# The low part behind the sums, and another order of pairs, in the output product of a short-convolution layer

## The chip, the cores and the metric

The kernel runs on one core of one Trainium2 chip. The metric is device time in microseconds (us), the median of several executions of the whole program. A second figure, the span, comes from one profiled execution: the time from the first to the last recorded instruction. The engines that matter are TensorE (PE in the profile, with its weight loads as PEld), VectorE (DVE), ScalarE (ACT) and SyncE (SP), whose queue issues the transfers from device memory. Each engine works off its own queue of instructions in the order of the built program, and semaphores tell it when what another engine or a transfer must have finished is done.

## What is computed

The reference, cut to one layer as it is run here (256 tokens, model width D = 2048, inner width E = 4096):

```python
h = rmsnorm(x, norm_g)
shift, scale, gate = split(silu(c) @ ada_w + ada_b, 3)
h = h * (1 + scale) + shift
b_gate, c_gate, v, g = split(h @ w_in, 4)              # w_in: D x 4E
y = b_gate * causal_conv3(c_gate * v) * silu(g)        # 256 tokens x E
out = rmsnorm(x + gate * (y @ w_out), final_g)         # w_out: E x D
```

The two big products are `h @ w_in` and `y @ w_out`. Everything is float32 and the products must keep more than one reduced-precision pass gives.

## The kernel before

**Three products for one.** TensorE multiplies operands of the type `float32r`. So each float32 operand is split into a high part (a cast to `float32r`, on ScalarE) and a low part (the operand less its high part, on VectorE), and a product is the sum of three: high by high, high by low, low by high. For the weights this split is the work of `split`: `split_hi` (L341) casts a loaded tile of 128 x 2048 on ScalarE, `split_lo` (L346) subtracts on VectorE. `triple` (L695) issues the three matmuls, each 128 x 128 by 128 x 512.

**Stages.** First come the norms, the modulation and the product with `w_in` (lines up to L657), whose results `y` are kept split in 16 tiles, `ys[0]` to `ys[15]`; one tile holds a pair of 128-row blocks of E. Then comes `y @ w_out`. Its first half, output columns 0 to 1023, is the loop over `order` at the end of which the change sits; it takes the 16 pairs one by one. Its second half, columns 1024 to 2047, is the loop `for dc in range(2, 4)` behind it, with the accumulator tile `mm_o`.

**Plain pairs.** For a plain pair `j` (0 to 9) the loop loads a tile `raw_o` with the two blocks of `w_out` (`load_o`, L684, 1 MB), splits it, and issues 24 matmuls, 8 triples, into the accumulators `wide[0]` and `wide[1]` (`mm_w` in the profile).

**Seven-product pairs.** Pairs 10 to 15 (`SEVEN`) go through `seven`, which needs 7 triples, 21 matmuls, in place of 8, in the manner of Strassen: it multiplies sums of blocks by sums of tokens. The token sums (`form`) were made earlier in `token_forms`. The weight sums are made here. The tile `raw_o` is seen as four blocks of 128 x 512. VectorE makes four sums `s` of them (`sums_o`) in three instructions: one for two sums at once (L720, 128 x 1024), then L722 and L723 (128 x 512 each, each reading what the one before wrote). ScalarE casts blocks 1 to 3 as loaded (L721, 128 x 1536), VectorE takes their low part `bl` (L724), and then the four sums are split like any tile: a cast on ScalarE (L341, 128 x 2048) and a low part on VectorE (L346, 128 x 2048). Three of the seven triples use the blocks as loaded, four use the sums; they accumulate into `wide`, `p75` (`mm`), `p1` and `p6` (`mm` as well in the profile, since buffer numbers are left out).

**Gather.** When the last seven-product pair has been issued, `gather` (L738 to L746) adds the accumulators `p1`, `p6` and `p75` up: one copy on ScalarE (L742) and four additions of 128 x 512 on VectorE (L741). The last three additions read `p75`. The accumulator `mm_o` of the next stage takes the place in PSUM that `p75` had, so its first matmul must wait for the last of them.

**Buffers.** The working tiles lie in nine buffers of 128 x 2048, three each of the kinds `raw`, `hi` and `lo`, handed out in turn. In this loop `raw_o` and `sums_o` take `lo` buffers, high parts take `hi` buffers, low parts take `raw` buffers. A plain pair so uses one buffer of each kind, a seven-product pair two of each. A load waits until the last reader of the third tile before it in its kind is done; a cast waits until TensorE has done with the third high part before.

**Order of the work.** A scheduler in the build orders the instructions of each engine from the order in which they are traced, their priorities and its own idea of their durations; what it has put down is then fixed. `tc.add_manual_dep(a, b, ...)` with the class `NoSync` only says that `a` is to stand behind `b` on their engine, and adds no semaphore. The order of the pairs is written out by hand in `order`.

Of the kernel before, what the change touches and what calls it, by code (L numbers as in the profile page):

```python
# [8 lines left out]
F32 = mybir.dt.float32  # L9
F32R = mybir.dt.float32r  # L10
AF = mybir.ActivationFunctionType
ALU = mybir.AluOpType
# [105 lines left out]
def short_conv_layer(ctx: ExitStack, tc: tile.TileContext, x, c, norm_g, ada_w, ada_b, w_in, conv_w, w_out, final_g, out):  # L118
    nc = tc.nc
# [25 lines left out]
    def w_tile(kind, name, dtype=F32, i=None):  # L145

        if i is None:
            i = nth[kind] % 3
            nth[kind] += 1
        return wpool.tile([P, SLOT], dtype, tag=f"{kind}{i}", name=name, bufs=1)  # L150
# [12 lines left out]
    after = mybir.DependencyInfo(mybir.DependencyClass.NoSync, mybir.DependencyReason.DATA)  # L163
# [111 lines left out]
    for t in range(TT):  # L275
        for dh in range(2):
# [3 lines left out]
            else:  # L280
                nc.vector.scalar_tensor_tensor(
                    out=junk[:, t], in0=xt[t][dh], scalar=1.0, in1=xt[t][dh], op0=ALU.mult, op1=ALU.mult,
# [50 lines left out]
    def hi_tile():  # L333
        return w_tile("hi", "hi", F32R)

    def lo_tile(lo_tag="lo"):
        return w_tile(lo_tag, "lo", F32R)
# [23 lines left out]
    def split(raw, n, lo_tag="lo"):  # L361

        return split_lo(raw, n, split_hi(raw, n), lo_tag)
# [64 lines left out]
    sums = {}  # L428
# [139 lines left out]
    def gate(dc):  # L568
        return gates[dc // 2][:, dc % 2, :]
# [119 lines left out]
    def y_parts(ct, t):  # L689
        return [ys[ct // 2][:, ct % 2, h, t * P : (t + 1) * P] for h in range(2)]  # L690

    def triple(dst, y, hi, lo, opens=False, ends=False):

        for i, (a, b) in enumerate(((0, hi), (0, lo), (1, hi))):
            nc.tensor.matmul(dst, y[a], b, start=opens and i == 0, stop=ends and i == 2, skip_group_check=True)  # L695
# [17 lines left out]
    def seven(j, raw):  # L713


        opens, last = j == SEVEN[0], j == SEVEN[-1]
        sums = w_tile("lo", "sums_o")
        hi, lo = hi_tile(), lo_tile("raw")
        b, s, bh, bl = (v.rearrange("p (b f) -> p b f", f=W) for v in (raw, sums, hi, lo))
        nc.vector.tensor_tensor(out=s[:, 0:2], in0=b[:, 1:3], in1=b[:, 0:1].to_broadcast([P, 2, W]), op=ALU.subtract)  # L720
        nc.scalar.copy(bh[:, 1:4], b[:, 1:4])  # L721
        nc.vector.tensor_tensor(out=s[:, 2], in0=b[:, 2], in1=s[:, 0], op=ALU.add)  # L722
        nc.vector.tensor_tensor(out=s[:, 3], in0=b[:, 3], in1=s[:, 2], op=ALU.subtract)  # L723
        nc.vector.tensor_tensor(out=bl[:, 1:4], in0=b[:, 1:4], in1=bh[:, 1:4].bitcast(F32), op=ALU.subtract)  # L724
        sh, sl = (v.rearrange("p (b f) -> p b f", f=W) for v in split(sums, SLOT, "raw"))

        def f(i):
            return [forms[j][h][:, i] for h in range(2)]

        triple(p1, y_parts(2 * j, 0), bh[:, 1], bl[:, 1], opens, last)  # L730
        triple(wide[0][:, 1], y_parts(2 * j + 1, 0), bh[:, 3], bl[:, 3])
        triple(wide[0][:, 0], f(3), bh[:, 2], bl[:, 2])
        triple(p75[:, 0], f(2), sh[:, 1], sl[:, 1], opens, last)
        triple(p75[:, 1], f(0), sh[:, 0], sl[:, 0], opens, last)
        triple(p6, f(1), sh[:, 2], sl[:, 2], opens, last)
        triple(wide[1][:, 1], y_parts(2 * j + 1, 1), sh[:, 3], sl[:, 3])
# [8 lines left out]
        add(ends[0][:, 0], p75[:, 1], u2)  # L745
        add(ends[1][:, 0], p75[:, 1], ends[1][:, 1])  # L746

    order = (0, 1, 10, 2, 11, 3, 12, 4, 13, 5, 14, 6, 15, 7, 8, 9)
    for n, j in enumerate(order):
        raw = w_tile("lo" if n else "raw", "raw_o")  # L750
        load_o(raw, 2 * j, 2, 0, 2 * W)
        load_ends(n - 4)
        if j in SEVEN:
            seven(j, raw)
            if j == SEVEN[-1]:
                gather()
            continue
        hi, lo = split(raw, SLOT, "raw")
        for t in range(TT):
            for k in range(2):  # L760
                for d in range(2):
                    o = slice((k * 2 + d) * W, (k * 2 + d + 1) * W)
                    triple(
                        wide[t][:, d], y_parts(2 * j + k, t), hi[:, o], lo[:, o],
                        n == 0 and k == 0, j == order[-1] and k == 1,
                    )
# [24 lines left out]
    for dc in range(2, 4):  # L791
# [16 lines left out]
        for ep in range(n_ep):  # L808
# [3 lines left out]
            if dc == 3:  # L812
# [3 lines left out]
                    out=raw3, in0=raw3, in1=gate(dc).unsqueeze(1).to_broadcast([P, EP, W]), op=ALU.mult  # L816
# [45 lines left out]
```

## Time and profile before

| what | us |
|---|---|
| median of three executions (911.7 to 912.86) | 911.83 |
| the profiled execution, its own time | 911.95 |
| span of that execution | 910.2 |
| TensorE busy in the span | 894.2 |
| VectorE busy | 653.5 |
| ScalarE busy | 476.1 |

How to read the views: a timeline row gives the start of an instruction in us from the start of the span, its duration, engine, line of the kernel, operation, what it writes and reads without buffer numbers, and in square brackets how long its engine had been idle before it and what ended that. "x2" merges two neighbours of a kind. A windows row gives the busy time and number of instructions of each engine in a stretch, then the clock granted to TensorE and the share of the transfer engines. Matmuls overlap: the distance from start to start, and not the duration, is what one costs.

### The profile page before, as it was taken

The page shows a single profiled execution, that of the slowest core. Times are in us where ns is not written, and L with a number is a line of the kernel's source. Part 1 is how long each engine was busy: PE and PEld are TensorE (multiplying, and loading weights), DVE is VectorE, ACT ScalarE, POOL GpSimd, SP SyncE. Part 2 cuts the span into 40 slices and gives each one's busy share as a digit, 9 for nine tenths or more (in the row PEclk, how much of TensorE's full clock was granted, in tenths as well). Part 3 has the DMA queues.
Part 4 walks back from the last instruction along what each step waited for, and adds up shares of the span by engine and source line. Part 5 has one row for each costly group of instructions (what it writes and reads, how often), then busy time and mean ns, then how long its engine had stood idle before and what let it go on. Part 6 is the DMA issues. An engine that isn't in the chain of part 4 may idle for free.

```text
span 910.2 us, 16272 instructions
## 1 busy us (share of the span) xinstructions
PE 894.2 (98%) x7029; PEld 854.7 (94%) x7029; DVE 653.5 (72%) x647; ACT 476.1 (52%) x422; POOL 0.7 (0%) x6
## 2 busy tenths in 40 slices
PE   6999999999999999999999999999999999999996
PEld 4999999999999999999999999999999987788885
DVE  4889899889888886665555686555555577887882
ACT  6768866665558765643333434343444335544343
POOL 0000000000000000000000000000000000000000
PEclk9999999999999999999999999999999999999998
DMA  9999999999998686676666887656666486685542
GB/s 313 367 371 349 364 309 365 346 370 359 345 327 282 184 301 189 189 241 202 202 186 186 259 273 231 201 185 194 185 193 197 137 307 191 209 293 185 185 138 93
DMA packets 159656, 227.65 MB, mean 250 GB/s; under 512 B 5680, under 2 KB 104160, under 8 KB 159200
## 3 DMA queue, kind: packets, MB, share of 16 engines
q1 hardware_dynamic: 159456, 226.56, 75.7%
q8 instruction: 55, 0.90, 0.4%
q14 instruction: 17, 0.14, 0.0%
q10 hardware_dynamic: 128, 0.04, 0.0%
HBM read 224.49 MB, written 2.10 MB: 249 GB/s over the span
## 4 chain that ended last, share of the span: by engine, by line
PE 98%; ACT 1%; DMA 1%; ACTq 0%; issue 0%; DVE 0%
PE mm_b L471 38%; PE mm_s L471 38%; PE mm_o L695 10%; PE mm_w L695 7%; PE mm L695 2%; PE tp_idle L258 1%; DMA rows<-in_ada_b_dram 1%; PE sum L380 1%; PE ps_gate L596 0%; PE tp_g L461 0%; PE tp_x L310 0%; ACT hi L341 0%; ACT acc L492 0%; ACT hT L327 0%; ACT mm_s L504 0%; ACT big L787 0%
## 5 line engine op out<-in xcount | busy, mean ns | idle before, releaser
L471 PE MATMUL mm_s<-hT,hi 128*128 128x256 f32 x2048 | 350.4, 277 | 0.1
L471 PE MATMUL mm_b<-hT,hi 128*128 128x256 f32 x2048 | 349.4, 276 | 0.0
L471 PEld LDWEIGHTS mm_s<-hT,hi 128*128 128x128 f32 x2048 | 308.5, 188 | 1.0 <-ACT hT L327 0.3
L471 PEld LDWEIGHTS mm_b<-hT,hi 128*128 128x128 f32 x2048 | 308.2, 188 | 0.5 <-issue 0.5
L471 PE MATMUL mm_b<-hT,lo 128*128 128x256 f32 x1024 | 282.6, 276 | 0.0
L471 PE MATMUL mm_s<-hT,lo 128*128 128x256 f32 x1024 | 282.2, 277 | 0.0
L346 DVE TENSOR_TENSOR lo<-raw,hi 128x2048 fp32r<-128x2048 f32 (+1 forms) x66 | 148.0, 2243 | 113.6 <-ACT hi L341 113.2
L341 ACT CAST hi<-raw 128x2048 fp32r<-128x2048 f32 (+1 forms) x66 | 123.7, 1874 | 193.9 <-PE mm_b L471 152.6
L471 PEld LDWEIGHTS mm_b<-hT,lo 128*128 128x128 f32 x1024 | 192.2, 188 | 0.5 <-issue 0.5
L471 PEld LDWEIGHTS mm_s<-hT,lo 128*128 128x128 f32 x1024 | 191.7, 188 | 0.3 <-DVE lo L346 0.2
L346 DVE TENSOR_TENSOR lo<-raw_s,hi 128x2048 fp32r<-128x2048 f32 (+1 forms) x80 | 147.6, 1850 | 32.8 <-ACT hi L341 32.0
L341 ACT CAST hi<-raw_s 128x2048 fp32r<-128x2048 f32 (+1 forms) x80 | 124.0, 1559 | 72.9 <-PE mm_s L471 59.6
L454 DVE SCALAR_TENSOR_TENSOR gv<-at,silu_c,gv 128x512 f32<-128x512 f32 x105 | 78.6, 749 | 6.3 <-DMA at<-in_ada_w_dram 4.5
L341 ACT CAST hi<-raw_o 128x2048 fp32r<-128x2048 f32 x26 | 49.6, 1906 | 60.6 <-PE mm_o L695 36.6
L695 PE MATMUL mm_o<-hi,y 128*128 128x512 f32 x256 | 78.7, 389 | 0.0
L346 DVE TENSOR_TENSOR lo<-raw_o,hi 128x2048 fp32r<-128x2048 f32 x26 | 59.5, 2290 | 24.2 <-ACT hi L341 24.1
L492 ACT COPY acc<-mm_s 128x1024 f32<-128x1024 f32 x54 | 54.6, 1012 | 34.7 <-PE mm_s L471 34.7
L695 PE MATMUL mm_w<-hi,y 128*128 128x512 f32 x184 | 58.2, 390 | 0.0
L695 PEld LDWEIGHTS mm_o<-hi,y 128*128 128x128 f32 x256 | 48.0, 188 | 9.9
L695 PE MATMUL mm_o<-lo,y 128*128 128x512 f32 x128 | 49.5, 389 | 0.0
L593 DVE SCALAR_TENSOR_TENSOR gacc<-at_g,silu_c,gacc 128x512 f32<-128x512 f32 x60 | 45.0, 749 | 5.6 <-DMA at_g<-in_ada_w_dram 4.6
L695 PEld LDWEIGHTS mm_w<-hi,y 128*128 128x128 f32 x184 | 34.5, 188 | 7.7 <-ACT hi L341 0.2
(142 smaller groups left out, 512.6 us busy)
## 6 DMA issues: line engine op xcount, KB each, us to landing
raw<-in_sc_w_in_dram SPq DMA_DIRECT2D x64, 1024.0 KB, 5.6
raw_s<-in_sc_w_in_dram SPq DMA_DIRECT2D x47, 1024.0 KB, 8.5
raw_o<-in_sc_w_out_dram SPq DMA_DIRECT2D x32, 1024.0 KB, 5.1
at<-in_ada_w_dram SPq DMA_DIRECT2D x114, 256.0 KB, 8.4
raw_s<-in_sc_w_in_dram SPq DMA_DIRECT2D x33, 512.0 KB, 6.9
at_g<-in_ada_w_dram SPq DMA_DIRECT2D x32, 512.0 KB, 7.6
at<-in_ada_w_dram SPq DMA_DIRECT2D x6, 512.0 KB, 9.4
x<-in_x_dram SPq DMA_DIRECT2D x4, 512.0 KB, 6.1
```

What stands on the lines that cost most here:

```text
L258: nc.tensor.matmul(tp_idle, ident, ones[:, 0:1].to_broadcast([P, 512]), start=True, stop=True)
L341: nc.scalar.copy(hi[:, :n], raw[:, :n])
L346: nc.vector.tensor_tensor(out=lo[:, :n], in0=raw[:, :n], in1=hi[:, :n].bitcast(F32), op=ALU.subtract)
L380: nc.tensor.matmul(sums0[:, o * P : (o + 1) * P], rows[:, o // NK0, (o % NK0) * P : (o % NK0 + 1) * P], col.to_broadcast([P, P]), start=k ...
L454: nc.vector.scalar_tensor_tensor(out=gv, in0=at4[:, i], scalar=c_k, in1=gv, op0=ALU.mult, op1=ALU.add)
L471: mm = last_mm[0] = nc.tensor.matmul(dst, w, h[k], start=begins and left, stop=ends, skip_group_check=True)
L492: nc.scalar.copy(acc[ch, q], bank)
L593: nc.vector.scalar_tensor_tensor(out=ga, in0=at3[:, i, :], scalar=s, in1=ga, op0=ALU.mult, op1=ALU.add)
L695: nc.tensor.matmul(dst, y[a], b, start=opens and i == 0, stop=ends and i == 2, skip_group_check=True)
```

## The change

Two things, both in the first half of `y @ w_out`.

In `seven`, a dependency of the class `NoSync` puts the low part `bl` of the blocks as loaded (L724) behind the last of the three instructions that make the sums (L723). Before, the scheduler was free to set L724 between them.

In `order`, the six seven-product pairs and the ten plain ones follow each other otherwise. Before, from the third place on, they alternate strictly and three plain pairs stand at the end (7, 8, 9). After, two plain pairs stand together at 2, 3 and at 5, 6, the others alternate, and one plain pair (9) stands behind the last seven-product pair (15).

```diff
-        nc.vector.tensor_tensor(out=s[:, 3], in0=b[:, 3], in1=s[:, 2], op=ALU.subtract)
-        nc.vector.tensor_tensor(out=bl[:, 1:4], in0=b[:, 1:4], in1=bh[:, 1:4].bitcast(F32), op=ALU.subtract)
+        all_sums = nc.vector.tensor_tensor(out=s[:, 3], in0=b[:, 3], in1=s[:, 2], op=ALU.subtract)
+        low = nc.vector.tensor_tensor(out=bl[:, 1:4], in0=b[:, 1:4], in1=bh[:, 1:4].bitcast(F32), op=ALU.subtract)
+        tc.add_manual_dep(low.ins, all_sums.ins.name, after, reason="the sums' cast runs beside the low part")
...
-    order = (0, 1, 10, 2, 11, 3, 12, 4, 13, 5, 14, 6, 15, 7, 8, 9)
+    order = (0, 1, 10, 2, 3, 11, 4, 12, 5, 6, 13, 7, 14, 8, 15, 9)
```

The number of loads, casts, additions and matmuls is the same in both. In the built program of after, the VectorE queue reads so from pair 13 on (the pair in brackets):

```
L724 low part as loaded (13), L346 low part of sums (13),
L720 first sums (14), L346 low part (7), L722 (14), L723 (14), L724 (14), L346 low part of sums (14),
L720 first sums (15), L346 low part (8), L722 (15), L723 (15), L724 (15), L346 low part of sums (15),
L346 low part (9), first addition of gather, L346 low part (first tile of mm_o),
second and third addition of gather, L346 low part (second tile of mm_o), last addition of gather
```

For the earlier pairs L720 stands behind the low part of the plain pair before it, as it does throughout in before. In before, all four additions of `gather` stand together, behind the low parts of pairs 7 and 8 and ahead of that of pair 9.

## Prediction

> **What bounds the kernel now.** I read the page first, then the busy time by windows, then the timelines of TensorE, VectorE and ScalarE through the stage that the change touches, and last the transfers.
>
> ```profile
> span 910.2 us, 16272 instructions
> ...
> PE 894.2 (98%) x7029; PEld 854.7 (94%) x7029; DVE 653.5 (72%) x647; ACT 476.1 (52%) x422; POOL 0.7 (0%) x6
> ...
> PEclk9999999999999999999999999999999999999998
> ...
> PE 98%; ACT 1%; DMA 1%; ACTq 0%; issue 0%; DVE 0%
> ```
>
> TensorE is the bound, nearly without a gap and at full clock, and the chain that ended last lies on it. So the edit is worth what it adds to or takes from TensorE's waits. The windows show where there are any:
>
> ```profile
> 760.00:770.00 10.00, 9.97 (x43) 7.72 (x42) 7.92 (x6) 5.19 (x3) 0.00 (x0) 1.00 0.58 186
> 780.00:790.00 10.00, 10.00 (x43) 7.75 (x43) 7.92 (x7) 5.19 (x3) 0.00 (x0) 1.00 0.62 204
> 800.00:810.00 10.00, 10.00 (x46) 8.26 (x45) 9.13 (x7) 3.95 (x3) 0.00 (x0) 1.00 0.89 319
> 900.00:910.00 10.00, 2.74 (x13) 1.93 (x11) 2.62 (x6) 3.74 (x8) 0.00 (x0) 0.75 0.59 211
> ```
>
> Where pairs alternate, TensorE issues 43 matmuls in 10 us, later 46: small stalls that "busy" hides, since matmuls overlap. The timeline sizes them:
>
> ```profile
> 730.63 0.39 PE L695 MATMUL mm_w<-hi,y 128*128 128x512 f32 x1
> ...
> 754.68 0.40 PE L695 MATMUL mm<-lo,form 128*128 128x512 f32 x1
> ...
> 786.55 0.50 PE L695 MATMUL mm<-lo,form_g 128*128 128x512 f32 x1
> ...
> 797.23 0.50 PE L695 MATMUL mm<-lo,form_h 128*128 128x512 f32 x1
> ...
> 810.55 0.39 PE L695 MATMUL mm_o<-hi,y 128*128 128x512 f32 x1
> ...
> 815.54 0.39 PE L695 MATMUL mm_w<-hi,y 128*128 128x512 f32 x1
> 815.77 0.39 PE L695 MATMUL mm_o<-lo,y 128*128 128x512 f32 x1
> ...
> 820.53 0.39 PE L695 MATMUL mm_o<-lo,y 128*128 128x512 f32 x1
> ```
>
> From 815.77 to 820.53 stand 21 matmuls without a wait: 0.2267 each. A plain pair is 24 of them, 5.44 us; a seven-product pair 21, 4.76. The stage, from 730.63 to 815.77, holds 10 x 24 + 6 x 21 = 366 and the one `mm_o` issued early, at 810.55: 367 x 0.2267 = 83.2 us, and takes 85.14. So its stalls come to **1.95 us**, and that is all there is to gain. They come with a period: from 786.55 to 797.23 a plain and a seven-product pair take 10.68 against 10.20.
>
> What sets 10.68 is a loop through VectorE and ScalarE:
>
> ```profile
> 745.91 1.22 DVE L720 TENSOR_TENSOR sums_o<-raw_o 128x1024 f32<-128x1024 f32 x1
> 747.17 0.69 DVE L722 TENSOR_TENSOR sums_o<-raw_o,sums_o 128x512 f32<-128x512 f32 x1
> ...
> 773.52 2.29 DVE L346 TENSOR_TENSOR lo<-sums_o,hi 128x2048 fp32r<-128x2048 f32 x1 [2.05 <-ACT hi L341]
> 775.73 2.28 DVE L346 TENSOR_TENSOR lo<-raw_o,hi 128x2048 fp32r<-128x2048 f32 x1
> 777.94 1.22 DVE L720 TENSOR_TENSOR sums_o<-raw_o 128x1024 f32<-128x1024 f32 x1
> 779.07 1.75 DVE L724 TENSOR_TENSOR lo<-raw_o,hi 128x1536 fp32r<-128x1536 f32 x1
> 780.74 0.69 DVE L722 TENSOR_TENSOR sums_o<-raw_o,sums_o 128x512 f32<-128x512 f32 x1
> 781.47 0.69 DVE L723 TENSOR_TENSOR sums_o<-raw_o,sums_o 128x512 f32<-128x512 f32 x1
> 784.20 2.29 DVE L346 TENSOR_TENSOR lo<-sums_o,hi 128x2048 fp32r<-128x2048 f32 x1 [2.05 <-ACT hi L341]
> ```
>
> ```profile
> 782.27 1.91 ACT L341 CAST hi<-sums_o 128x2048 fp32r<-128x2048 f32 x1 [3.98 <-DVE sums_o L723]
> ...
> 787.44 1.48 ACT L721 CAST hi<-raw_o 128x1536 fp32r<-128x1536 f32 x1 [1.47 <-DMA raw_o<-in_sc_w_out_dram]
> ...
> 815.97 1.91 ACT L341 CAST hi<-raw_o 128x2048 fp32r<-128x2048 f32 x1 [3.76 <-PE mm_w L695]
> ```
>
> VectorE works 8.63 us of a period and stands idle 2.05, while ScalarE casts the sums (1.91). From 773.52 to 784.20 is the same 10.68 as TensorE's.
>
> **The low part behind the sums.** Nothing is added or removed: L724 (1.75) now runs beside the cast. The sums go 1.26 (745.91 to 747.17), 0.73, then L724 starts 0.60 after L723; the cast starts 0.11 after L723's end and ends 0.69 + 0.11 + 1.91 = 2.71 after its start, L724 at 2.35. VectorE's idle time falls from 2.05 to 0.4, its period to about 9.1, below the 10.20 that TensorE needs. That takes the 1.95 away. Nothing waits longer for L724 itself: TensorE reads it first among the pair's low parts, but the sums were what came late. What is late next is a transfer, below.
>
> **The order of the pairs.** Matmuls, casts and loads are as many as before and the 16 loads keep their places on SP's queue. Plain pairs put earlier give VectorE room (2.2 us for 5.44 of TensorE). Two new things come in at the end, both out of the order in which the VectorE queue is built.
>
> *First wait: the low part of pair 8.* In the queue of after, L720 of pairs 14 and 15 stands ahead of the low part of plain pairs 7 and 8. L720 waits for its load, and that load has the buffer which L724 of the pair before gives free. So a loop closes: L724 (14) ends, load (15), L720 (15), low part (8). The load:
>
> ```profile
> L684 SPq DMA_DIRECT2D raw_o<-in_sc_w_out_dram x32: 367/368/379, 707.8 to 875.2; - x32
> ...
> DMA to landing us min/median/max: 5.0/5.1/7.6
> ```
>
> L723 ended at 781.47 + 0.69 = 782.16 and released a load whose cast began at 787.44: 5.28 for ScalarE. For VectorE I take 5.2. From L720 (14) to L720 (15): 1.13 + 2.21 + 0.73 + 0.60 + 1.75 + 5.2 = 11.6 us, where TensorE needs 10.2. VectorE's own sum of 9.1 no longer decides; it now idles for a transfer.
>
> Whether that shows depends on the lead before it, so I follow the chain from where it hangs on TensorE. Without stalls pair 3 ends after 117 matmuls, at 730.63 + 26.52 = 757.15, and frees the buffer for the cast of pair 4; a waiter starts 0.43 after the last matmul's start (815.54 to 815.97), so at 757.35. Then: low part (4) 1.95 later, 759.30; L720 (12) 761.51; L722 762.77; L723 763.50; L724 764.10, done 765.85; load of 6 and its cast 5.28 later, 771.13; low part (6) 773.06; L720 (13) 775.27; L724 (13) 777.86, done 779.61; load of 14; L720 (14) 784.81; low part (7) 785.94 to 788.23. TensorE wants it after another 135 matmuls from 757.15 and the three of pairs 7 and 14 that need no low part, at 788.43: just in time. A round later the low part (8) ends at 788.23 + 11.6 = 799.83 and is wanted at 788.43 + 10.20 = 798.63. **Wait: 1.2 to 1.3 us.**
>
> *Second wait: the accumulator of the next stage.* `mm_o` needs the place of `p75`, which `gather` reads. In before it was read long ahead:
>
> ```profile
> 804.30 0.68 DVE L741 TENSOR_TENSOR z<-mm,z 128x512 f32<-128x512 f32 x1
> 804.90 2.28 DVE L346 TENSOR_TENSOR lo<-raw_o,hi 128x2048 fp32r<-128x2048 f32 x1
> ```
>
> The last addition ended at 804.98, 5.6 before the first `mm_o` at 810.55. In after only pair 9 stands behind pair 15, and the last addition is queued behind the low parts of two tiles of the next stage. TensorE goes on at about 799.9, has 22 matmuls of pair 8 left (to 804.9), 20 of 15 and 24 of 9: ready for `mm_o` at 814.9. VectorE: cast of pair 9 when pair 8 ends, 805.1; low part (9) 807.0; first addition 809.2; low part 809.8 (or 0.2 later, for its own load); two additions at 812.2; low part 813.4; last addition 815.6, done 816.3. **Wait: 1.4 to 1.6 us.** Both waits start a matmul stream anew, which before costs 0.11 each time (matmuls of 0.50 at 786.55 and 797.23 against 0.39).
>
> **The sum.** 1.3 + 1.5 + 0.2 - 1.95 = +1.05. On the profiled execution, 911.95, that is 913.0; on the median, which is 0.12 lower, **912.9 us** (+0.12%). Behind `mm_o`'s first matmul VectorE and ScalarE have slack, so it is all there is.
>
> The load's time carries both signs. With 5.0, the least that the trace has, both rounds shorten by 0.1 or 0.2: first wait 1.0, sum +0.7. The Trainium skill ("DMA: Bandwidth & Descriptors", Anatomy of one DMA) fits a transfer as about 2.0 us and its bytes at 436 GB/s, measured for transfers that GpSimd issues; an estimate from it for 1 MB is 4.4 us, by which the first wait would vanish and the sum be -0.35, so 911.5. This case's loads take 5.0 to 5.2 where they stand alone, so the trace decides. The other end is crowded loads:
>
> ```profile
> L684 SPq DMA_DIRECT2D raw_o<-in_sc_w_out_dram x1: 367/367/367, 802.5 to 802.5; - x1
> ...
> DMA to landing us min/median/max: 6.5/6.5/6.5
> ```
>
> **The rivals.**
>
> *Crowded loads, slower.* The load of 15 is issued about 3 us behind that of 8, and the first of the next stage 3 us behind that of 9. If the distance is too short, each is up to 6.5 - 5.1 = 1.4 late, and adds that to its wait: +1.05 + 2.8 = up to 915.7, and 914.2 if it is half. It decides from 0.4 us each on, where the sum passes 0.2%. For it: the row above, behind another load. Against: loads 4 us apart took 5.1. Chance 0.25.
>
> *One wait only.* If the load is 0.6 quicker than I take it, or the lead at pair 7 is a microsecond more, the first wait goes: -1.95 + 1.5 + 0.1, 911.5. It is where the fit of the Trainium skill leads. Against: the chain hangs on TensorE and on rows that repeat. Chance 0.10.
>
> *Neither wait, faster.* The dependency does what it is for and TensorE catches up with nothing: 911.83 - 1.95 = 909.9. It needs the last addition of `gather` 1.5 earlier, against its place in the queue. Chance 0.05.
>
> *The clock falls after a wait.* The window from 900 shows 0.75 where TensorE stands idle most of the time; 2.5 us in 10. After each of two waits that would be +5: 918. Against: stalls in before leave 1.00. Chance 0.02. The Trainium skill ("TensorE: Matmul & The Clock Gate", HAM oscillation) speaks of idle gaps over about 3.4 us, which these are not.
>
> That the dependency does nothing is excluded: in the built queue L724 stands behind L723 in all six pairs.
>
> **How the numbers follow.** 0.2% of 911.83 is 1.8 us, about what a measurement of this kernel tells from no change. My forecast has 0.58, with its own range 912.3 to 913.6. Within 0.2% lie it, less a little at its upper end, and the one-wait case: 0.65. Slower are the crowded loads, the clock and that upper end: 0.30. Faster: 0.05. The range runs from the one-wait case, 911.3, to the crowded loads at somewhat over half, 914.5, and leaves out the faster case, the clock and the worst of the loads.
>
> **What would show it.** VectorE's wait before the low part of the sums near 0.4 in place of 2.05; no stalls of TensorE through pair 13; one of 1.2 to 1.3 at the first low part of pair 8, VectorE having waited over 2 us for a load before L720 of 14 and 15; one of 1.4 to 1.6 before the first `mm_o`. I am wrong if the load of 15 takes over 5.5, if pair 7 already waits, or if a wait of TensorE stands in a place not named here.

## The result and the profile after

The changed kernel takes 914.18 us in the median, against 911.83 before: a ratio of 1.0025, with a 95% interval from 1.0017 to 1.0034. So it is slower by 2.35 us, a quarter of a per cent. (One execution of 2351.95 us is left out.) The profiled execution took 914.21 us with a span of 912.4.

First the page of after, the chain that ended last, by engine:

```profile
PE 88%; DMA 5%; DVE 3%; ACT 2%; issue 1%; SPq 1%; ACTq 0%; DVEq 0%
```

Before, 98% of it lay on TensorE; now it leaves TensorE and runs through transfers, VectorE and ScalarE. These shares say what the chain runs through, not how long TensorE waits, which is far less. They say that TensorE waits somewhere, and that what it waits for hangs on a load. The windows of after say where (columns as before: busy time and count for TensorE, its weight loads, VectorE, ScalarE and GpSimd, then clock and transfers):

```profile
760.00:770.00 10.00, 10.00 (x46) 8.29 (x45) 8.35 (x7) 4.12 (x3) 0.00 (x0) 1.00 0.67 213
...
810.00:820.00 10.00, 8.16 (x35) 6.15 (x34) 10.00 (x10) 5.67 (x5) 0.00 (x0) 1.00 0.83 278
```

From 760 to 770 TensorE issues 46 matmuls where it issued 43: the small stalls are gone. Later there are real gaps, and from 810 to 820 VectorE is busy all the time while TensorE issues 35. The timeline of TensorE in after sizes them (in after the lines of `gather` stand one lower, so L742 is the addition that was L741):

```profile
730.05 0.39 PE L695 MATMUL mm_w<-hi,y 128*128 128x512 f32 x1
...
787.64 0.39 PE L695 MATMUL mm<-hi,y 128*128 128x512 f32 x1
788.25 0.50 PE L695 MATMUL mm_w<-lo,y 128*128 128x512 f32 x1 [0.23 <-DVE lo L346]
...
798.36 0.39 PE L695 MATMUL mm<-hi,y 128*128 128x512 f32 x1
800.04 0.50 PE L695 MATMUL mm_w<-lo,y 128*128 128x512 f32 x1 [1.30 <-DVE lo L346]
...
809.51 0.86 PE L695 MATMUL mm_w<-hi,y 128*128 128x512 f32 x3
810.61 0.50 PE L695 MATMUL mm_w<-lo,y 128*128 128x512 f32 x1 [0.24 <-DVE lo L346]
...
815.50 0.39 PE L695 MATMUL mm_w<-hi,y 128*128 128x512 f32 x1
817.50 0.47 PE L695 MATMUL mm_o<-hi,y 128*128 128x512 f32 x1 [1.60 <-DVE z L742]
```

From 730.05 to 787.64 lie 254 steps of 0.2267 us, 57.58 in 57.59: no stall up to pair 13 and into pair 7. Then four waits. Each is the distance from the start before, less 0.2267: 0.38 at pair 7, 1.45 at pair 8, 0.42 at pair 9 (the last of the three at 809.51 starts at 809.96) and 1.77 at the first `mm_o`: 4.02. With the restarts and some hundredths, the stage's 366 matmuls (82.97) take 87.45 from 730.05 to 817.50, so 4.48 stand beside them where 1.95 stood. That is 2.53 more. TensorE reached the stage 0.58 earlier (730.05 against 730.63; a second trace of after, below, has 730.46, so this varies from one execution to the next) and what is behind it took 0.24 longer; together 2.2, as the spans say.

The timeline of VectorE in after, with L724 of pair 12 and then the end of the stage:

```profile
763.56 1.75 DVE L724 TENSOR_TENSOR lo<-raw_o,hi 128x1536 fp32r<-128x1536 f32 x1
...
784.77 1.22 DVE L720 TENSOR_TENSOR sums_o<-raw_o 128x1024 f32<-128x1024 f32 x1 [2.66 <-DMA raw_o<-in_sc_w_out_dram]
785.91 2.28 DVE L346 TENSOR_TENSOR lo<-raw_o,hi 128x2048 fp32r<-128x2048 f32 x1
...
789.44 1.75 DVE L724 TENSOR_TENSOR lo<-raw_o,hi 128x1536 fp32r<-128x1536 f32 x1
791.58 2.29 DVE L346 TENSOR_TENSOR lo<-sums_o,hi 128x2048 fp32r<-128x2048 f32 x1 [0.38 <-ACT hi L341]
796.56 1.23 DVE L720 TENSOR_TENSOR sums_o<-raw_o 128x1024 f32<-128x1024 f32 x1 [2.70 <-DMA raw_o<-in_sc_w_out_dram]
797.71 2.28 DVE L346 TENSOR_TENSOR lo<-raw_o,hi 128x2048 fp32r<-128x2048 f32 x1
```

The dependency does its work: 0.38 idle before the low part of the sums at 791.58, where 2.05 stood. But VectorE now stands 2.66 and 2.70 before L720 of pairs 14 and 15, for their loads, and the low parts of pairs 7 and 8 are queued behind it. What ScalarE did at that time shows what this costs (the timeline of ScalarE in after):

```profile
770.94 1.91 ACT L341 CAST hi<-raw_o 128x2048 fp32r<-128x2048 f32 x1 [1.78 <-DMA raw_o<-in_sc_w_out_dram]
...
793.61 1.91 ACT L341 CAST hi<-raw_o 128x2048 fp32r<-128x2048 f32 x1 [2.07 <-PE mm_w L695]
...
806.32 1.91 ACT L341 CAST hi<-raw_o 128x2048 fp32r<-128x2048 f32 x1 [2.98 <-DMA raw_o<-in_sc_w_out_dram]
```

The high part of pair 8 was ready at 793.61 + 1.91 = 795.52, and its low part started at 797.71, though VectorE had nothing to do until 796.56. The Trainium skill ("TensorE: Matmul & The Clock Gate", Architectural detail: the array is 16x 32x32, not 1x 128x128) calls the queues of ScalarE and VectorE strictly first in, first out; this trace agrees, with an idle engine for 1.04 us ahead of work that was ready.

The fourth wait is at `gather`. VectorE in after, from the low part of pair 9 to the last addition:

```profile
808.26 2.29 DVE L346 TENSOR_TENSOR lo<-raw_o,hi 128x2048 fp32r<-128x2048 f32 x1 [2.59 <-ACT hi L341]
...
811.07 2.28 DVE L346 TENSOR_TENSOR lo<-raw_o,hi 128x2048 fp32r<-128x2048 f32 x1
813.27 1.28 DVE L742 TENSOR_TENSOR z<-mm,big 128x512 f32<-128x512 f32 x2
814.47 2.28 DVE L346 TENSOR_TENSOR lo<-raw_o,hi 128x2048 fp32r<-128x2048 f32 x1
816.66 0.68 DVE L742 TENSOR_TENSOR z<-mm,z 128x512 f32<-128x512 f32 x1
```

VectorE has no idle time from 808.26 on. Its last addition ends at 816.66 + 0.68 = 817.34, behind the low parts of two tiles of the next stage, and the first `mm_o` starts at 817.50.

### The profile page after: what moved, and what is told of

Its sections match the earlier page's. It is cut to its first block, busy times and chain, and to the rows that moved or that the text cites. A ratio compares the mean times of both kernels' runs of the same rounds, so it can differ in the third digit from the quotient of the medians.

```text
span 912.4 us, 16272 instructions
## 1 busy us (share of the span) xinstructions
PE 892.8 (98%) x7029; PEld 854.9 (94%) x7029; DVE 653.6 (72%) x647; ACT 476.9 (52%) x422; POOL 0.7 (0%) x6
## 4 chain that ended last, share of the span: by engine, by line
PE 88%; DMA 5%; DVE 3%; ACT 2%; issue 1%; SPq 1%; ACTq 0%; DVEq 0%
PE mm_b L471 38%; PE mm_s L471 36%; PE mm_o L695 10%; PE mm_w L695 3%; DMA raw_o<-in_sc_w_out_dram 2%; DMA raw_s<-in_sc_w_in_dram 2%; DVE lo L346 1%; ACT hi L341 1%; DMA at<-in_ada_w_dram 1%; SPq L231 1%; DMA x<-in_x_dram 1%; DVE lo L724 1%; PE ps_gate L596 0%; PE tp_g L461 0%; PE mm L695 0%
```

## The experiments

Theory A, from the prediction: two places in VectorE's built queue cost the time, L720 ahead of the low part of pairs 7 and 8 (first wait), and the last addition of `gather` behind two low parts (second wait). The dependency by itself is a gain. The rivals blame the order of pairs itself, through loads that come closer together, or the dependency. Where a kernel's timeline is shown, the first `mm_w` and the first `mm_o` bound the stage; 82.97 of what lies between is matmuls.

### Each half alone

The dependency with the old order:

```diff
-    order = (0, 1, 10, 2, 3, 11, 4, 12, 5, 6, 13, 7, 14, 8, 15, 9)
+    order = (0, 1, 10, 2, 11, 3, 12, 4, 13, 5, 14, 6, 15, 7, 8, 9)
```

> The dependency alone, with the order of pairs of before. Theory A (the dependency takes the stalls away, the order of the pairs puts new ones in): no stall of TensorE in the stage, since VectorE's period falls to about 9.1 us against TensorE's 10.2, L720 stands behind the low part of the plain pair throughout, and three plain pairs stand behind the gather; 911.83 - 1.95 = 909.9, between 909.4 and 910.4. Theory B (the late low part of the blocks as loaded is itself what costs, because TensorE reads it first in a pair): the small stalls only move to the first low part of each seven-product pair, 911.8 or above.

Measured: 910.21 us, ratio to before 0.9981 (0.9972 to 0.9990). TensorE's timeline:

```profile
730.39 0.39 PE L695 MATMUL mm_w<-hi,y 128*128 128x512 f32 x1
...
813.42 0.39 PE L695 MATMUL mm_o<-hi,y 128*128 128x512 f32 x1
```

83.03 us, so no wait is left. The dependency is worth 1.6 us, close to the 1.95 of stalls that there were to gain.

The new order without the dependency:

```diff
-        tc.add_manual_dep(low.ins, all_sums.ins.name, after, reason="the sums' cast runs beside the low part")
```

> The order of pairs alone, without the dependency. Theory A: pairs 7 and 8 still wait, since in the built queue the first sums of 14 and 15 stand ahead of their low parts here too (0.5 to 0.8 and about 1.6 us), pair 9 perhaps 0.5; the first mm_o does not, since here the last addition of gather stands behind one tile of the next stage and not two; with no small stalls of the strict alternation left or only a few: 912.2 to 913.2. Theory B: without the dependency the loss goes, 911.2 to 911.9.

Measured: 913.22 us, ratio 1.0017 (1.0008 to 1.0026), at the upper end of what theory A had. Its profiled execution was 1.9 us above that median, so its rows are read for places, not sizes. First VectorE, then TensorE, then windows of the same stretch:

```profile
798.42 1.23 DVE L720 TENSOR_TENSOR sums_o<-raw_o 128x1024 f32<-128x1024 f32 x1 [4.11 <-DMA raw_o<-in_sc_w_out_dram]
```

```profile
798.85 0.84 PE L695 MATMUL mm_w<-hi,y 128*128 128x512 f32 x3
799.95 0.50 PE L695 MATMUL mm<-hi,y 128*128 128x512 f32 x1 [0.26 <-ACT hi L721]
801.90 0.50 PE L695 MATMUL mm_w<-lo,y 128*128 128x512 f32 x1 [1.44 <-DVE lo L346]
...
818.68 0.39 PE L695 MATMUL mm_o<-hi,y 128*128 128x512 f32 x1
```

```profile
799.00:802.00 3.00, 1.30 (x6) 0.53 (x4) 3.00 (x3) 0.90 (x1) 0.00 (x0) 1.00 0.00 0
803.00:806.00 3.00, 3.00 (x8) 2.32 (x7) 1.72 (x2) 1.17 (x1) 0.00 (x0) 0.50 0.87 289
```

The wait for the load before L720 (15) is there without the dependency: it belongs to the order. (It is longer than in after, partly because the load of 15, issued 2.3 us behind that of pair 8, took 6.7 us here and 5.3 in after.) The wait before `mm_o` is not there: the row has no idle time. In this built queue the last three additions of `gather` stand together behind one low part of the next stage; in after the last stands behind two. So the two halves don't add up (-1.6 and +1.4 give +2.35): the scheduler builds another queue for the two together, and only that one has the second wait.

Its TensorE waits 0.93 at pair 7 and 1.72 at pair 8, as theory A has it. But what put this execution above the median is mostly the clock. Behind waits of 0.42 and 1.72 us with one matmul between, the clock granted to TensorE fell from 1.00 to 0.50, and from 803 to 806 it issued 8 matmuls where after issued 15. From 802.70 to 806.34 it started 9 matmuls, which at full clock take 2.04 us in place of 3.64: about 1.6 of the 1.9. Its mean granted clock, 0.996, is also the lowest of the eleven executions of this kernel.

### Each wait alone

L720 placed behind the low part of the pair ahead, all else as in after:

```diff
+    low_op = [None]
...
-        nc.vector.tensor_tensor(out=lo[:, :n], in0=raw[:, :n], in1=hi[:, :n].bitcast(F32), op=ALU.subtract)
+        low_op[0] = nc.vector.tensor_tensor(out=lo[:, :n], in0=raw[:, :n], in1=hi[:, :n].bitcast(F32), op=ALU.subtract).ins
...
-        nc.vector.tensor_tensor(out=s[:, 0:2], in0=b[:, 1:3], in1=b[:, 0:1].to_broadcast([P, 2, W]), op=ALU.subtract)
+        first = nc.vector.tensor_tensor(out=s[:, 0:2], in0=b[:, 1:3], in1=b[:, 0:1].to_broadcast([P, 2, W]), op=ALU.subtract)
+        tc.add_manual_dep(first.ins, low_op[0].name, after, reason="the low part of the pair ahead first")
```

> After, and the first sums of a seven-product pair (L720) stand behind the low part of the pair ahead; with it the scheduler also sets three of the four additions of gather together and the last behind one tile of the next stage. Theory A: no wait at pairs 7, 8 and 9 and none before mm_o, at most 0.3 at a cast: 910.0 to 910.6. Theory C (the new order costs by itself, through crowded loads or buffers, whatever stands where on VectorE): 912 or above.

Measured: 910.36 us, ratio 0.9986 (0.9977 to 0.9995). VectorE, then TensorE (lines are shifted by two or more here):

```profile
795.30 2.29 DVE L348 TENSOR_TENSOR lo<-raw_o,hi 128x2048 fp32r<-128x2048 f32 x1 [1.20 <-ACT hi L341]
...
812.02 0.68 DVE L745 TENSOR_TENSOR z<-mm,z 128x512 f32<-128x512 f32 x1
```

```profile
730.32 0.39 PE L697 MATMUL mm_w<-hi,y 128*128 128x512 f32 x1
...
813.53 0.39 PE L697 MATMUL mm_o<-hi,y 128*128 128x512 f32 x1
```

The low part of pair 8 starts 2.4 us earlier than in after, right behind its cast, and L720 behind it, at 797.51, waits for nothing. The stage takes 83.21 us: all four waits are gone. The one before `mm_o` is gone for two reasons. VectorE comes to `gather` earlier (its first addition starts at 807.90; in after it started at 810.47), and the last addition, the row at 812.02, now stands behind the low part of one tile and not two. The first alone would not do: with the 6.87 us that `gather` took in after from its first addition to its last, it would end at 814.77, behind the 813.53 at which `mm_o` starts here. The order of pairs costs nothing by itself that these times can tell.

The last addition of `gather` ahead of the low part of the first tile of `mm_o`, all else as in after (`low_op` notes the last low part in `split_lo`, as in the run before; L720 stays where it was):

```diff
...
-        add = lambda out, a, b: nc.vector.tensor_tensor(out=out, in0=a, in1=b, op=ALU.add)
+        def add(out, a, b):
+            gathered[0] = nc.vector.tensor_tensor(out=out, in0=a, in1=b, op=ALU.add).ins.name
...
+            if dc == 2 and ep == 0:
+                tc.add_manual_dep(low_op[0], gathered[0], after, reason="the accumulator first")
```

> After, and the low part of the first tile of mm_o stands behind the last addition of gather; nothing else in VectorE's queue ahead of it changes. Theory A: the wait of 1.85 us before the first mm_o goes and those at pairs 7, 8 and 9 stay: 914.18 - 1.85 = 912.3, between 912.0 and 912.7. Theory D (mm_o waits for its own tile as much as for the accumulator): the wait stays or only changes its name, 913.8 to 914.5.

Measured: 912.38 us, ratio 1.0005 (0.9996 to 1.0014). TensorE:

```profile
730.77 0.39 PE L697 MATMUL mm_w<-hi,y 128*128 128x512 f32 x1
...
800.34 0.50 PE L697 MATMUL mm_w<-lo,y 128*128 128x512 f32 x1 [1.18 <-DVE lo L348]
...
815.50 0.39 PE L697 MATMUL mm_o<-hi,y 128*128 128x512 f32 x1
```

The wait at pair 8 stays and the one at `mm_o` is gone: 84.73 us, 1.76 beside the matmuls. But theory A had the waits at pairs 7 and 9 stay too, and here pair 7 waits 0.07 and pair 9 not at all, though nothing ahead of them in VectorE's queue was changed. From after to here are 1.8 us of medians, about the second wait's 1.77; from here to the run before are 2.0. So the waits at the two places cost about as much, and the second can be cured by itself.

### The rest of the order

L720 placed as above, but without the dependency:

```diff
+        tc.add_manual_dep(first.ins, low_op[0].name, after, reason="the low part of the pair ahead first")
...
-        tc.add_manual_dep(low.ins, all_sums.ins.name, after, reason="the sums' cast runs beside the low part")
```

> The new order with the first sums of a seven-product pair behind the low part of the pair ahead, but without the dependency: against the run with both it tells what the dependency is worth once no load stands in the way. Theory A (VectorE's period, 10.68 against 10.20, still counts, but the two plain pairs set early give a lead of some 2 us that four alternating pairs use up at 0.48 each): no stalls until late in the stage, 0.3 to 1.2 us in all at pairs 15, 9 or the first mm_o, 910.7 to 911.6. Rival (the order alone is enough, the dependency is worth nothing there): 910.2 to 910.5. Rival (the dependency is worth its 1.6 in any order): 911.9 or more.

Measured: 911.07 us, ratio 0.9992 (0.9983 to 1.0001). VectorE, then TensorE:

```profile
793.60 2.29 DVE L348 TENSOR_TENSOR lo<-sums_o,hi 128x2048 fp32r<-128x2048 f32 x1 [2.05 <-ACT hi L341]
```

```profile
730.54 0.39 PE L697 MATMUL mm_w<-hi,y 128*128 128x512 f32 x1
...
814.39 0.47 PE L697 MATMUL mm_o<-hi,y 128*128 128x512 f32 x1 [0.16 <-DVE z L744]
```

VectorE's 2.05 are back and 0.88 of waits stand in the stage, against 0.24 with the dependency; the medians differ by 0.7. Theory A had 910.7 to 911.6. So plain pairs set early do give VectorE a lead, and in this order the dependency has less left to give than in the old one (1.6).

After with two plain pairs behind the last seven-product pair:

```diff
-    order = (0, 1, 10, 2, 3, 11, 4, 12, 5, 6, 13, 7, 14, 8, 15, 9)
+    order = (0, 1, 10, 2, 3, 11, 4, 12, 5, 13, 6, 14, 7, 15, 8, 9)
```

> After with only the tail of its order changed: 5, 13, 6, 14, 7, 15, 8, 9 in place of 5, 6, 13, 7, 14, 8, 15, 9. The two plain pairs 2, 3 still stand together, the dependency stays, and two plain pairs stand behind the last seven-product pair. In the built queue no first sums (L720) stand ahead of a low part of a plain pair, and the additions of gather come earlier by a pair. Theory A (both waits come from how the VectorE queue is built at the tail): no waits, 910.1 to 910.5, span 908.4 to 908.8. Rival (setting plain pairs together costs by itself, through the loads that come closer): at least half of the 1.6 to 4 us that after lost stays, 911.5 or more.

Measured: 910.45 us, ratio 0.9984 (0.9975 to 0.9993). From the first `mm_w`, 730.49, to the first `mm_o`, 813.73, are 83.24 us. The 0.27 beside the matmuls are a stall of 0.07 and its restart at 772.51, in pair 13, and some hundredths; the four waits of after are gone, though pairs 2 and 3 still stand together. In this built queue L720 stands behind the low part of the pair ahead all through the loop's end. Moving one plain pair is enough.

After itself once more, for a second trace:

> After itself once more, for a second profile. Theory A (the first wait is the loop through a load, and the wait at pair 9 was one load that took 6.2 in that execution): pair 8 again 1.2 to 1.6 and the first mm_o 1.5 to 1.8; at pair 9 a wait only if its load takes over 5.7. Rival (the load of pair 9 is regularly late in this order): again 5.8 or more and 0.3 to 0.5 at pair 9.

Measured: 914.7 us in one execution. TensorE, and the load of pair 9:

```profile
788.04 0.39 PE L695 MATMUL mm<-hi,y 128*128 128x512 f32 x1
788.33 0.50 PE L695 MATMUL mm_w<-lo,y 128*128 128x512 f32 x1
...
800.09 0.50 PE L695 MATMUL mm_w<-lo,y 128*128 128x512 f32 x1 [1.26 <-DVE lo L346]
...
810.79 0.51 PE L695 MATMUL mm_w<-lo,y 128*128 128x512 f32 x1 [0.38 <-DVE lo L346]
```

```profile
L684 SPq DMA_DIRECT2D raw_o<-in_sc_w_out_dram x1: 368/368/368, 800.1 to 800.1; - x1
...
DMA to landing us min/median/max: 6.4/6.4/6.4
```

Pair 8 waits again, 1.26 by its row (1.30 in the first trace), and so does the first `mm_o`, 1.79 (1.77). At pair 7 only 0.06: TensorE had entered the stage 0.41 later, and the low part came 0.08 later. Pair 9 waits again, and its load took 6.4 (6.2 in the first trace). So the rival was right for these two traces: that load is late in both. In the run with `gather` first, where nothing ahead of it in the queue differs, the same load took 5.6 and pair 9 did not wait. So the wait at pair 9 comes and goes with that load; what makes the load late is not shown.

## Why the prediction was right and where it was wrong

The time, 914.18, lies in the range, but above the 912.3 to 913.6 that the likeliest case was given, and just beyond the 0.2% that was to count as no change, on the side that had a chance of 0.30. The mechanism was right in its two places; the size was not. The forecast's +1.05 is measured as +2.35 in the medians and +2.53 in the stage of the profiled execution. That the time still lies in the range is owed to the room that the range left for crowded loads. And two of the signs of being wrong that the prediction named did come: pair 7 waited, and a wait stood in a place that it had not named, at pair 9.

- *The dependency.* VectorE's idle time 0.38 (forecast 0.4), no stalls through pair 13, -1.95: right, and shown alone by the first experiment, with -1.6 in the medians.
- *The first wait* stood in its place, and the run that puts L720 behind the low part takes it away. Its size was under-estimated: 1.3 forecast, 0.38 + 1.45 measured. The chain of the prediction had pair 7 "just in time"; it was late. The failing term is the load. I took 5.28 from the end of L724 of pair 12 to the cast of pair 6; measured are 763.56 + 1.75 to 770.94, 5.63. From L724 to L720 I took 5.2; measured are 5.34 and 5.37 (789.44 + 1.75 to 796.56). The three come to 0.66 and the excess of the wait, its first restart of 0.11 counted in, to 0.64. That this shows at pair 7 or at pair 8 hangs on when TensorE enters the stage, as the second trace showed.
- *The second wait* was right in its place and cause too, 1.77 against 1.4 to 1.6. The forecast left out the 0.16 from the end of the last addition, 817.34, to the start of `mm_o`.
- *The wait at pair 9*, 0.42, was not forecast. I let its cast start when pair 8 frees the buffer; it waited for the load, issued at 800.0 and landed at 806.2, and started at 806.32. The same lateness brought VectorE later to `gather`, but TensorE too, so that it added little to the second wait.
- *The restarts* cost 0.39 for four, not 0.2 for two.
- *Crowded loads*, the rival, was half right. It looked at the load of 15, which took 5.3, and at the first of the next stage, 5.9. The first was on time, and the lateness of the second cost nothing, since VectorE had no idle time from 808.26 on. What cost were the late loads of pairs 6 and 9. The rival had 914.2 for half the crowding, which is where the time came out; that is luck.
- *The clock.* In after it stayed at 1.00 behind every wait: the longest, 1.77, left 1.00 in the window from 810 to 820. But the rival is real: in the profiled execution of the order alone the granted clock fell to 0.50 for some 3 us, behind waits of 0.42 and 1.72. The Trainium skill ("TensorE: Matmul & The Clock Gate", HAM oscillation) speaks of gaps over about 3.4 us; after agrees with it, and the order alone does not, since its waits were shorter. What set that fall off, where the 1.77 of after did not, stays open.

The other rivals (one wait, or neither) fell. Neither wait is what the two kernels with another queue or another tail show, at 910.36 and 910.45. Of the kernels here the old order with the dependency has the lowest median, 910.21, but the three lie too close to be told apart.

## What to carry to other kernels

Where a scheduler orders a queue, read the built queue: an instruction that waits for a load, set ahead of one that is ready, puts the load into the loop, above all when the load's buffer is freed by that same engine. The effects of two changes need not add up, because the queue is built anew for the two together: here it got a wait that neither change has alone. And when a chain is "just in time", count each transfer in it at more than its time alone.

## What was unexpected of the hardware

Between 745 and 832 us, in all runs, the loads of 1 MB took from 4.9 to 5.4 us where no other was issued within 3.5 us, with one exception below, and up to 7.2 where one was issued 2.2 to 3.2 us ahead or behind. That of pair 6 in after, issued at 765.3, took 5.5, and that of pair 13, 2.7 behind it:

```profile
L684 SPq DMA_DIRECT2D raw_o<-in_sc_w_out_dram x1: 368/368/368, 768.0 to 768.0; - x1
...
DMA to landing us min/median/max: 6.9/6.9/6.9
```

But distance doesn't tell it all. In the run of the dependency alone a load with none issued for 4.2 us ahead of it and 6.0 behind took 6.5, the exception:

```profile
L684 SPq DMA_DIRECT2D raw_o<-in_sc_w_out_dram x1: 368/368/368, 770.4 to 770.4; - x1
...
DMA to landing us min/median/max: 6.5/6.5/6.5
```

TensorE did not wait for it. The load issued at 800.0 in after had none ahead of it for 8.8 us and one 3.0 behind, and took 6.2; that at 788.2, also with one 3.0 behind, took 5.1; and with `gather` first the load at 800.3, with the same neighbours, took 5.6. What makes such a load late stays open. The fit in the Trainium skill ("DMA: Bandwidth & Descriptors", Anatomy of one DMA) gives 4.4 as an estimate for 1 MB, for transfers that GpSimd issues; no load of this stage, issued by SyncE, was that quick.
